# One relation of SBUF places, modulo 256 bytes, for the K steps of a float32 transformer layer

## The chip, the cores and the metric

The kernel runs on one core of one Trainium2 chip. The metric is the device time of one execution in microseconds: the median of three executions is 1042.79 us (1042.51 to 1045.53). TensorE (PE) multiplies, ScalarE (ACT) and VectorE (DVE) prepare operands, GpSimd (POOL) helps with elementwise work, SyncE (SP) issues most transfers. SBUF is the on-chip memory that the engines read, 128 partitions wide; a "place" in this document is the byte at which an operand starts within its partition.

## The reference, cut to what matters

One decoder layer over 272 tokens (16 meta tokens ahead of 256), model width 2048, all in float32:

```
p = h @ w_in                       -> q heads | kv latent | indexer q, k, weights | pool channels
A = sparse attention (top-64 keys of a lightning indexer, T5 bias, shared latent KV)
B = multi-scale causal pooling of the pool channels, a linear map per group, a scale
h = LN(alpha*h + concat(A, B) @ w_o)
z = conv3(h @ w_up) + b;  f = (gelu(z_a) * z_g) @ w_down          (w_up: 2048 x 11264, w_down: 5632 x 2048)
h = LN(alpha*h + f);  the 256 real tokens are returned
```

## The kernel before, in words

**Products in two parts.** Float32 values are split into an upper part (rounded to float32r by ACT) and a lower part (the rest, by DVE), and a product is three TensorE products: upper weights by upper activations, lower weights by upper activations, upper weights by lower activations. `product` (L256 to L265) does this for one block of 128 output columns: 16 K steps of 128 rows each, and in each step three matmuls, L263 (`wh`, `ah`), L264 (`wl`, `ah`), L265 (`wh`, `al`). A matmul holds a 128x128 weight block in the array (the trace shows its load as LDWEIGHTS on PEld, just before the matmul) and streams 256 to 272 activation columns past it. While one matmul streams, the block of the next one is loaded; so PE reads two places of SBUF at once: the activations of this matmul and the weights of the next.

**The stream of weights.** All weights come as tiles of 128 x 2048 floats in one fixed order, the list `stream`: items 0 to 7 are the indexer's queries, 8 and 9 the latent maps, 10 to 17 the query heads, 18 to 25 the pool channels, 26 to 41 the output projection, and from 42 on the plan of `ffn_plan`: 88 "up" items (one per block of 128 columns of `w_up`) with "down" items (`w_down`) between them. `fetch` (L162) brings an item by one DMA on SP into a `wraw` tile and splits it by two ACT (L158) and two DVE (L159) instructions into a `whl` tile. `wraw` and `whl` have three buffers each, so an item is fetched and split while PE uses those ahead of it. Down items go through `seven` (L849 on; matmuls L860 to L862), where activations are held in the array and 512 weight columns stream.

**Where operands lie.** A `whl` tile has 4352 floats, 17408 bytes, which is 68 x 256. The upper part starts at the first of `places(n)`, the lower at the second, both in floats from the tile's start; a step's block is 512 bytes behind the last, so it has the same place modulo 256. Activations of a K step (`xp`: the input, `mixa` and `mixp`: the mixers' outputs, `hp`: the normalised rows) lie in the `ring` pool in slots of 576 floats, 2304 bytes, 9 x 256. In the built program both pools start at 96 modulo 256, so the relation of two operands modulo 256 follows from the offsets alone.

- `places(n)` (L99) gives item n the upper place 4*(n % 16) floats, which is 16 bytes further for each item, and the lower one 2048 + s floats behind it, where s goes through `SHIFTS` = 0, 12, 24, 36, 52 as n // 16 goes up. For an up item n is its number among the up items plus 72 (`order_of`, L136 to L139); other items take their number in the stream.
- `Parts` (L82) puts an activation tile's upper part at float 0 and its lower at 272 for the first eight K blocks of the order `K_UP`, and at 2 and 276 for the last eight (`ACTS`). `xp` tiles are plain (L286): upper at 0, lower 288 floats behind; indexer queries read them from token 16, query heads from token 14, pool channels from token 0, 6, 10 or 12.

The first 8 up items use other activations, `fold` tiles (L728, 2080 bytes each, so that each starts 32 bytes further modulo 256 than the one before it), because the layer norm is folded in later. The 80 others use `hp`, of which 16 x 80 = 1280 K steps follow.

As an example: up item 71 has n = 143, so its upper weights lie at 4*15 = 60 floats and its lower 2048 + 36 floats behind; up item 87 has n = 159, upper again at 60 floats, lower 2048 + 52 behind.

Of the kernel before, what the change touches and what calls it, by code (L numbers as in the profile page):

```python
# [12 lines left out]
F32R = mybir.dt.float32r  # L13
# [68 lines left out]
class Parts:  # L82


    def __init__(self, slot, k):
        flat = slot.rearrange("p a b -> p (a b)")
        (a, b) = ACTS[k in K_UP[8:]]
        self.parts = flat[:, a:a + NQ], flat[:, b:b + NQ]

# [4 lines left out]
WIDE = 288  # L94
ACTS = ((0, 272), (2, 276))
SHIFTS = (0, 12, 24, 36, 52)


def places(n):  # L99

    upper = 4 * (n % 16)
    return upper, upper + 2048 + SHIFTS[n // 16 % 5]

# [7 lines left out]
def tile_layer(ctx, tc, xt, w_first, w_proj, w_uk, w_uv, w_pool, w_o, w_up, w_down, cols, rows, rel_bias, onehot, out):  # L111
# [23 lines left out]
    plan = ffn_plan()  # L135
    kinds, order_of, n_up = {}, {}, 0  # L136
    for item in plan:
        if item[0] == "up":
            order_of[len(stream)] = n_up + 72  # L139
            n_up += 1  # L140
            stream.append(w_up[item[2] * FT + item[1]])
        elif item[0] == "down":
            n = PARTS[FAST]
            stream.append(w_down[sum(PARTS[:FAST]) + n // 2 + (item[2] - 1) // 2 * (n // 4) + item[3]])
        else:
            kinds[len(stream)] = item[0]
            stream.append(w_down[sum(PARTS[:item[1]]) + item[2] * (PARTS[item[1]] // 2) + item[3]])
# [42 lines left out]
    def emit(i):  # L190
# [14 lines left out]
        if i == spare:  # L205
            raw = wp.tile([P, 2048], F32, tag="wraw", name="wraw")
            hl = Split(sb.tile([P, 4160], F32R, tag="y", name="whl_y"), 0, 2056)
        else:
            raw, hl = weight_tiles((0, 2112) if i > spare else places(order_of.get(i, i)))
        ready[i] = hl  # L210
# [61 lines left out]
    for k0, k1 in [(k, k + 1) for k in range(9)] + [(9, 12), (12, 15), (15, 16)]:  # L272
# [10 lines left out]
        for k in range(k0, k1):  # L283
            xk, wk, a0 = raw[:, k % 3, :T], raw[:, k % 3, T:], k % 6 // 3 * 1024 + k % 3 * MF
            c = slice(a0, a0 + MF)
            a = ring.tile([P, 2, T], F32R, tag="act", name="xp", padded_shape=[P, 2, WIDE])  # L286
            nc.scalar.activation(a[:, 0, :], xk, AF.Copy)
            nc.scalar.activation(hl[:, 0, c], wk, AF.Copy)
            nc.vector.tensor_tensor(a[:, 1, :], xk, a[:, 0, :].bitcast(F32), op=ALU.subtract)
            nc.vector.tensor_tensor(hl[:, 1, c], wk, hl[:, 0, c].bitcast(F32), op=ALU.subtract)  # L290
            x_parts.append(a)
            first.append((hl, c.start))
# [302 lines left out]
    def values(h, pts, ptx):  # L595
# [4 lines left out]
        nc.tensor.matmul(ps[:, 2 + P:NQ], vs[2][:, hs], pts[:, 2 * P:], start=False, stop=True)  # L600
        a = Parts(ring.tile([P, 2, WIDE], F32R, tag="act", name="mixa"), h)
        nc.scalar.activation(a[:, 0, :NQ], ps[:, :NQ], AF.Copy)
# [35 lines left out]
    def pooled(g, df, hl):  # L638
        for j in range(2):
# [6 lines left out]
            m = 2 * g + j  # L646
            a = Parts(ring.tile([P, 2, WIDE], F32R, tag="act", name="mixp"), 8 + m)
            nc.scalar.activation(a[:, 0, :NQ], ps[:, :NQ], AF.Copy, scale=col(G_POOL, m))
# [125 lines left out]
    def normalise(m):  # L774
        yd = y[:, m, Q0:]
        nc.vector.tensor_tensor(yd, yd, rs, op=ALU.mult)
        nc.vector.tensor_tensor(yd, yd, m2, op=ALU.add)
        nc.scalar.activation(yd, yd, AF.Identity, bias=col(LN1, 2 * m + 1), scale=col(LN1, 2 * m))
        a = Parts(ring.tile([P, 2, WIDE], F32R, tag="act", name="hp"), m)
        nc.scalar.activation(a[:, 0, :NQ], yd, AF.Copy)  # L780
        nc.vector.tensor_tensor(a[:, 1, :NQ], yd, a[:, 0, :NQ].bitcast(F32), op=ALU.subtract)  # L781
        h_parts.append(a)
# [377 lines left out]
```

## Time and profile before

| | us |
|---|---|
| median of three executions | 1042.79 |
| the profiled execution | 1042.49 |
| its span, first to last instruction | 1040.7 |
| PE busy in the span | 1033.0 |
| DVE busy | 890.9 |
| ACT busy | 620.6 |

Durations of PE matmuls overlap in the trace (one starts about 0.12 us behind the last and is shown for 0.28 us), so what a matmul costs is read from the distance between starts: in a timeline the first column is the start, the second the duration, both in us. One K step is the distance from one L263 to the next. In a table of windows each row is one stretch of time: its length, then each engine's busy time and number of instructions, the granted TensorE clock, the DMA engines' share and the rate in GB/s. The clock is a share of full speed there; over the whole span its mean is 0.997.

### The profile page before, as it was taken

Reading aid. Unit: us, or ns where it says so; the run is one execution under the profiler, and the core shown is the slowest. Engines: PE = TensorE matmul, PEld = TensorE weight load, DVE = VectorE, ACT = ScalarE, POOL = GpSimd, SP = SyncE. Lnnn points to the kernel's source line nnn. Section 1 sums busy time; section 2 is a strip of 40 time slices with the busy share of each in tenths; the row PEclk is TensorE's granted clock in tenths of the full one; section 3 lists DMA queues with packets and bytes.
Section 4 is the critical chain, followed back from the end, with each engine's and each line's share of the span. In section 5 each row is a group of like instructions: output and inputs, shape, how many; then the busy total and the mean of one; then the engine's idle time right before and its main releaser. Section 6 shows DMA issues by size and latency. Waiting matters only on the chain.

```text
span 1040.7 us, 19199 instructions
## 1 busy us (share of the span) xinstructions
PE 1033.0 (99%) x7644; PEld 983.8 (95%) x7644; DVE 890.9 (86%) x1401; ACT 620.6 (60%) x1000; POOL 185.5 (18%) x245
## 2 busy tenths in 40 slices
PE   9999999999999999999999999999999999999997
PEld 8999999999999999999999999999999999999986
DVE  6879668758779998888989989989998999989876
ACT  7656456645439845565656556565556565566665
POOL 1200014125320021120121101211112111120031
PEclk9999999999999999999999999999999999999998
DMA  9755643454554578978887788887888779887765
GB/s 326 261 186 194 236 144 132 135 200 162 185 181 140 190 224 242 282 282 288 287 270 266 275 291 273 277 266 270 298 274 278 263 276 287 277 273 269 286 214 161
DMA packets 59754, 250.28 MB, mean 240 GB/s; under 512 B 21734, under 2 KB 22416, under 8 KB 32656
## 3 DMA queue, kind: packets, MB, share of 16 engines
q1 hardware_dynamic: 34592, 230.42, 61.5%
q0 software_dynamic: 7888, 16.14, 8.2%
q10 hardware_dynamic: 17184, 2.49, 1.4%
q8 instruction: 60, 0.98, 0.4%
q14 instruction: 30, 0.25, 0.1%
HBM read 232.50 MB, written 2.11 MB: 225 GB/s over the span
## 4 chain that ended last, share of the span: by engine, by line
PE 94%; issue 2%; DMA 1%; DVE 1%; POOL 1%; ACT 0%; SPq 0%; POOLq 0%; DVEq 0%; ACTq 0%
PE mm L263 24%; PE mm L265 24%; PE mm L264 24%; PE at L861 6%; PE at L860 6%; PE at L862 6%; PE mm L336 2%; DMA wraw<-in_w_down 1%; DVE whl L159 1%; POOL gb L979 0%; PE mm L564 0%; DMA wraw<-in_w_first 0%; PE at L599 0%; PE at L425 0%; PE at L426 0%
## 5 line engine op out<-in xcount | busy, mean ns | idle before, releaser
L159 DVE TENSOR_TENSOR whl<-wraw,whl 128x1024 fp32r<-128x1024 f32 (+1 forms) x416 | 486.4, 1204 | 40.5 <-ACT whl L158 39.5
L158 ACT ACTIVATE whl<-wraw 128x1024 fp32r<-128x1024 f32 (+1 forms) x416 | 402.6, 1014 | 102.1 <-DMA wraw<-in_w_up 21.9
L263 PE MATMUL mm<-hp,whl 128*128 128x258 f32 x1280 | 362.4, 283 | 0.0
L264 PE MATMUL mm<-hp,whl 128*128 128x258 f32 x1280 | 361.5, 282 | 0.0
L265 PE MATMUL mm<-hp,whl 128*128 128x258 f32 x1280 | 361.5, 282 | 0.0
L264 PEld LDWEIGHTS mm<-hp,whl 128*128 128x128 f32 x1280 | 242.6, 190 | 3.1
L263 PEld LDWEIGHTS mm<-hp,whl 128*128 128x128 f32 x1280 | 242.1, 189 | 3.1
L265 PEld LDWEIGHTS mm<-hp,whl 128*128 128x128 f32 x1280 | 242.1, 189 | 0.4 <-DVE hp L781 0.2
L263 PE MATMUL mm<-xp,whl 128*128 128x256 f32 (+5 forms) x384 | 111.7, 291 | 0.0
L265 PE MATMUL mm<-xp,whl 128*128 128x256 f32 (+5 forms) x384 | 108.6, 283 | 0.0
L264 PE MATMUL mm<-xp,whl 128*128 128x256 f32 (+5 forms) x384 | 108.4, 282 | 0.0
L795 ACT ACTIVATE z<-mm,cv 128x256 f32<-128x256 f32 x40 | 22.6, 565 | 99.6 <-PE mm L265 99.6
L832 POOL TENSOR_TENSOR forms<-za 128x128 f32<-128x128 f32 x20 | 21.2, 1061 | 311.0 <-DVE za L813 244.5
L263 PEld LDWEIGHTS mm<-xp,whl 128*128 128x128 f32 x384 | 72.3, 188 | 0.6
L264 PEld LDWEIGHTS mm<-xp,whl 128*128 128x128 f32 x384 | 72.4, 188 | 0.4
L265 PEld LDWEIGHTS mm<-xp,whl 128*128 128x128 f32 x384 | 72.2, 188 | 0.5 <-issue 0.5
L795 ACT ACTIVATE za<-mm,cv 128x256 f32<-128x256 f32 x40 | 22.6, 565 | 83.4 <-PE mm L265 75.1
L861 PE MATMUL at<-whl,gp 128*128 128x512 f32 x180 | 70.8, 394 | 0.0
L862 PE MATMUL at<-whl,gp 128*128 128x512 f32 x180 | 70.6, 393 | 0.0
L860 PE MATMUL at<-whl,gp 128*128 128x512 f32 x180 | 69.2, 394 | 0.0
L835 POOL TENSOR_TENSOR forms<-za 128x128 f32<-128x128 f32 x20 | 20.3, 1016 | 199.9 <-DVE za L813 199.9
L862 PEld LDWEIGHTS at<-whl,gp 128*128 128x128 f32 x180 | 33.8, 188 | 7.7
(349 smaller groups left out, 1885.9 us busy)
## 6 DMA issues: line engine op xcount, KB each, us to landing
wraw<-in_w_up SPq DMA_DIRECT2D x88, 1024.0 KB, 5.1
wraw<-in_w_down SPq DMA_DIRECT2D x80, 1024.0 KB, 6.7
wraw<-in_w_proj SPq DMA_DIRECT2D x24, 1024.0 KB, 5.2
wraw<-in_w_o SPq DMA_DIRECT2D x16, 1024.0 KB, 4.9
y<-v POOLq DMA_DIRECT2D x27, 256.0 KB, 8.0
y<-u POOLq DMA_DIRECT2D x18, 256.0 KB, 4.9
wraw<-in_w_first SPq DMA_DIRECT2D x8, 304.0 KB, 5.3
x<-in_xt SPq DMA_DIRECT2D x1, 2176.0 KB, 8.2
```

Of the source, the lines that this page charges most:

```text
L158: upper = nc.scalar.activation(hl[:, 0, c], raw[:, c], AF.Copy)
L159: lower = nc.vector.tensor_tensor(hl[:, 1, c], raw[:, c], hl[:, 0, c].bitcast(F32), op=ALU.subtract)
L263: nc.tensor.matmul(ps, wh, ah, start=n == 0, stop=False)
L264: nc.tensor.matmul(ps, wl, ah, start=False, stop=False)
L265: nc.tensor.matmul(ps, wh, al, start=False, stop=n == KT - 1)
L336: nc.tensor.matmul(ps[:m, :T], hl[:, t // 2, a0 + a:a0 + a + m], x_parts[k][:, t % 2, :], start=k == 0 and t == 0, stop=k == KT - 1 and t ...
L795: nc.scalar.activation(z, src[:, 2:NQ], AF.Identity, bias=col(C_B, j), scale=col(C_W, 3 * j + 2))
L832: nc.gpsimd.tensor_tensor(s[:, 0], a21, a22, op=ALU.add)
L835: nc.gpsimd.tensor_tensor(s[:, 3], a11, a21, op=ALU.subtract)
L860: nc.tensor.matmul(ps, a[:, 0, i], hl[:, 0, w], start=j == 0, stop=False)
L861: nc.tensor.matmul(ps, a[:, 0, i], hl[:, 1, w], start=False, stop=False)
L862: nc.tensor.matmul(ps, a[:, 1, i], hl[:, 0, w], start=False, stop=j == n - 1)
```

## The change

`places` gives three fixed upper places instead of a sweep: 10 floats for items 0 to 7, 8 floats for items 8 to 25, 60 floats for all others, up and down items alike. The lower part is 2084 floats (8336 bytes) behind the upper one everywhere. `Parts` takes its offset and width as arguments: `xp` tiles now start at float 0, `mixa`, `mixp` and `hp` at float 2, and the lower part is always 274 floats (1096 bytes) behind the upper. The number, order, engine and size of all instructions and transfers stay as they are, and so do the tiles.

```
-        (a, b) = ACTS[k in K_UP[8:]]
-        self.parts = flat[:, a:a + NQ], flat[:, b:b + NQ]
+        self.parts = [flat[:, a:a + width] for a in (first, first + 274)]
...
-ACTS = ((0, 272), (2, 276))
-SHIFTS = (0, 12, 24, 36, 52)
+SHIFT = 36
+LATE, EARLY, QUERY = 60, 8, 10
...
 def places(n):
-    upper = 4 * (n % 16)
-    return upper, upper + 2048 + SHIFTS[n // 16 % 5]
+    upper = QUERY if n < 8 else EARLY if n < 26 else LATE
+    return upper, upper + 2048 + SHIFT
...
-            raw, hl = weight_tiles((0, 2112) if i > spare else places(order_of.get(i, i)))
+            raw, hl = weight_tiles((0, 2112) if i > spare else places(i))
...
-            a = ring.tile([P, 2, T], F32R, tag="act", name="xp", padded_shape=[P, 2, WIDE])
+            a = Parts(ring.tile([P, 2, WIDE], F32R, tag="act", name="xp"), 0, T)
...
-        a = Parts(ring.tile([P, 2, WIDE], F32R, tag="act", name="mixa"), h)
+        a = Parts(ring.tile([P, 2, WIDE], F32R, tag="act", name="mixa"), 2, NQ)
...
-        a = Parts(ring.tile([P, 2, WIDE], F32R, tag="act", name="hp"), m)
+        a = Parts(ring.tile([P, 2, WIDE], F32R, tag="act", name="hp"), 2, NQ)
```

`mixp` is changed like `mixa`, and the bookkeeping of `order_of` and `n_up` goes.

More of the change, by code (lines that the diff above doesn't have):

```diff
@@ L82, with __init__ @@
 class Parts:
-    def __init__(self, slot, k):
+    def __init__(self, slot, first, width):
         flat = slot.rearrange("p a b -> p (a b)")
-        (a, b) = ACTS[k in K_UP[8:]]
-        self.parts = flat[:, a:a + NQ], flat[:, b:b + NQ]
+        self.parts = [flat[:, a:a + width] for a in (first, first + 274)]
     def __getitem__(self, key):
@@ L135, in tile_layer @@
     plan = ffn_plan()
-    kinds, order_of, n_up = {}, {}, 0
+    kinds = {}
     for item in plan:
         if item[0] == "up":
-            order_of[len(stream)] = n_up + 72
-            n_up += 1
             stream.append(w_up[item[2] * FT + item[1]])
@@ L646, in pooled @@
             m = 2 * g + j
-            a = Parts(ring.tile([P, 2, WIDE], F32R, tag="act", name="mixp"), 8 + m)
+            a = Parts(ring.tile([P, 2, WIDE], F32R, tag="act", name="mixp"), 2, NQ)
             nc.scalar.activation(a[:, 0, :NQ], ps[:, :NQ], AF.Copy, scale=col(G_POOL, m))
```

## The prediction

> **What bounds the kernel now.** I read the page first, its busy times and its chain of waits.
>
> ```profile
> span 1040.7 us, 19199 instructions
> ...
> PE 1033.0 (99%) x7644; PEld 983.8 (95%) x7644; DVE 890.9 (86%) x1401; ACT 620.6 (60%) x1000; POOL 185.5 (18%) x245
> ...
> PE 94%; issue 2%; DMA 1%; DVE 1%; POOL 1%; ACT 0%; SPq 0%; POOLq 0%; DVEq 0%; ACTq 0%
> PE mm L263 24%; PE mm L265 24%; PE mm L264 24%; PE at L861 6%; PE at L860 6%; PE at L862 6%; PE mm L336 2%; DMA wraw<-in_w_down 1%; DVE whl L159 1%; POOL gb L979 0%; PE mm L564 0%; DMA wraw<-in_w_first 0%; PE at L599 0%; PE at L425 0%; PE at L426 0%
> ```
>
> PE is the bound: 94% of the chain, 72% of it in the three matmuls of a K step. So the question is how fast these run one behind the other. Windows over stretches that hold little else say that: query heads, output projection, the first eight up items on `hp`.
>
> ```profile
> 92.00:138.10 46.10, 46.10 (x386) 45.96 (x385) 30.47 (x61) 18.97 (x26) 0.00 (x0) 1.00 0.51 182
> 220.32:301.40 81.08, 81.08 (x677) 81.03 (x676) 61.39 (x72) 39.53 (x59) 33.11 (x31) 1.00 0.52 181
> 349.32:395.50 46.18, 46.18 (x386) 46.00 (x385) 42.96 (x82) 27.93 (x47) 8.75 (x13) 1.00 0.69 208
> ```
>
> The counts take in matmuls that only reach into a window. The first and third hold 8 products, 384 matmuls: 46.10 / 128 K steps is 360.2 ns a step, 46.18 / 128 is 360.8. The second holds 14 products, 224 steps: 81.08 / 224 is 362. The clock is at 1.00 and the load of weights fills all but a little of the time, yet PE never idles: what can change is only the rate of the steps. I call the mean of a step before 360.5 ns.
>
> **The change, its main part.** In bytes and modulo 256, weights less activations, the change fixes the three pairs that PE reads at once. While L264 streams (upper activations), the upper weights for L265 load: 240 - 8 = 232 for `hp` and the mixers, 40 - 64 = 232 for indexer queries (token 16 is 64 bytes in), 32 - 56 = 232 for query heads. While L263 streams, the lower weights load: 232 + 8336 gives 120. While L265 streams (lower activations, 1096 = 72 further), the next upper weights load: 232 - 72 = 160. So the triple is 120, 232, 160 in all 8 + 8 + 16 + 80 products.
>
> The trace of before holds this very triple once: the second half of up item 71 (upper weights at float 60, lower 2084 behind it, activations at floats 2 and 276). Here are the starts of its first step, its third, its last, and of what follows it:
>
> ```profile
> 850.10 0.28 PE L263 MATMUL mm<-hp,whl 128*128 128x258 f32 x1
> ...
> 850.81 0.28 PE L263 MATMUL mm<-hp,whl 128*128 128x258 f32 x1
> ...
> 852.54 0.28 PE L263 MATMUL mm<-hp,whl 128*128 128x258 f32 x1
> ...
> 852.89 0.39 PE L860 MATMUL at<-whl,right 128*128 128x512 f32 x1
> ```
>
> Two steps take 0.71 us, 355 ns each; then six take 2.08 us, 346.7 ns each. The half that is nearest to it is the second half of up item 87, whose upper weights and activations lie the same, and whose lower weights lie 64 bytes further (triple 184, 232, 160):
>
> ```profile
> 981.23 0.28 PE L263 MATMUL mm<-hp,whl 128*128 128x258 f32 x1
> ...
> 981.95 0.28 PE L263 MATMUL mm<-hp,whl 128*128 128x258 f32 x1
> ...
> 984.11 0.39 PE L860 MATMUL at<-whl,right 128*128 128x512 f32 x1
> ```
>
> Its last six steps take 2.16 us, 360 ns each. So the fast pace is not that of the place 232 alone. Is it a property of the triple, or an accident of one half? The query heads say which, since their places before were constant over all 16 steps:
>
> ```profile
> 94.83 0.28 PE L263 MATMUL mm<-xp,whl 128*128 128x258 f32 x1
> ...
> 97.66 0.28 PE L263 MATMUL mm<-xp,whl 128*128 128x258 f32 x1
> ...
> 103.45 0.28 PE L263 MATMUL mm<-xp,whl 128*128 128x258 f32 x1
> ...
> 106.33 0.28 PE L263 MATMUL mm<-xp,whl 128*128 128x258 f32 x1
> ...
> 109.21 0.28 PE L263 MATMUL mm<-xp,whl 128*128 128x258 f32 x1
> ```
>
> The first of these two (item 10) runs its second half at 2.83 / 8 = 354 ns, the other (item 13) both of its halves at 2.88 / 8 = 360. The two halves of item 13 use ring slots of other places modulo 512 and agree, so 256 is enough of a period, and a pace once found is kept. I take the fast pace as the triple's own: two steps of 355 ns, then 346.7.
>
> - **Up items**, 80 products of 16 steps: after, 2 x 0.355 + 14 x 0.3467 = 5.56 us; before, 16 x 0.3605 = 5.77. 0.21 us each, **16.6 us** together.
> - **Output projection**, 16 products, the same triple and almost the same pace before: 16 x 0.21 = **3.3 us**.
> - **Query heads**, 8 products at 360.2 before: 8 x 0.20 = **1.6 us**.
> - **Indexer queries**, 8 products, the triple again but only 256 columns, which the trace does not show with it. Bounds from the nearest product, item 4 of the stream:
>
> ```profile
> 50.86 0.28 PE L263 MATMUL mm<-xp,whl 128*128 128x256 f32 x1
> ...
> 51.57 0.28 PE L263 MATMUL mm<-xp,whl 128*128 128x256 f32 x1
> 51.91 0.28 PE L263 MATMUL mm<-xp,whl 128*128 128x256 f32 x1
> ...
> 53.67 0.28 PE L263 MATMUL mm<-xp,whl 128*128 128x256 f32 x1
> ```
>
> Its eight steps take 351 ns each, single ones 340 (0.34 us). With 128 steps, between 351 to 340 (a gain of 1.4 us) and 351 to 360 (a loss of 1.2) I take a gain of 0.5, nearer to the fast end since the triple was fast at 258 columns.
>
> Sum: 16.6 + 3.3 + 1.6 + 0.5 = **22.0 us**.
>
> **The change, what else it moves.** *Down items* now stream weights from places 240 and 128 instead of many. Their activations stay spread over many places. Two of their steps, a fast one and a slow one:
>
> ```profile
> 705.92 0.40 PE L860 MATMUL at<-whl,right 128*128 128x512 f32 x1
> ...
> 706.63 0.40 PE L860 MATMUL at<-whl,right 128*128 128x512 f32 x1
> ...
> 862.13 0.39 PE L860 MATMUL at<-whl,gp 128*128 128x512 f32 x1
> ...
> 862.81 0.39 PE L860 MATMUL at<-whl,gp 128*128 128x512 f32 x1
> ```
>
> 0.71 and 0.68 us. If all 252 steps went from the middle to one end, that is 252 x 0.015 = 3.8 us either way; since the activations keep their spread I take 0 and keep 1 us each way. The 8 folded up items (moving relation) and the 8 pool products (four relations, mostly other widths) have 256 steps; by 6 ns either way (360 against the 354 of item 10) 1.5 us, taken as 0.
>
> *Splitting.* ACT and DVE write `whl` at other places. The whole of them, and the split of item 71, which wrote just the new places:
>
> ```profile
> L158 ACT ACTIVATE whl<-wraw x416: 609/1049/1086, 20.6 to 1009.1; 128x1024 fp32r<-128x1024 f32 x127, 128x512 fp32r<-128x512 f32 x12
> ...
> L159 DVE TENSOR_TENSOR whl<-wraw,whl x416: 677/1219/1668, 21.7 to 1011.4; 128x1024 fp32r<-128x1024 f32 x127, 128x512 fp32r<-128x512 f32 x12
> ...
> 840.60 2.01 ACT L158 ACTIVATE whl<-wraw 128x1024 fp32r<-128x1024 f32 x2 [0.92 <-DMA wraw<-in_w_up]
> ...
> 841.69 2.63 DVE L159 TENSOR_TENSOR whl<-wraw,whl 128x1024 fp32r<-128x1024 f32 x2
> ```
>
> ACT takes 2.01 us for the pair, twice its median (least, median, most ns) less their overlap; DVE takes 2.63 against 2.44 for two medians. At worst each of the 168 up and down items costs DVE 0.2 us more, 34 us in all, which lies beside PE; I take 0 and keep it for the cover.
>
> *Cover.* A faster PE asks for weights sooner. One of the DVE splits with least time to spare ends 1.2 us ahead of its use:
>
> ```profile
> 859.92 2.35 DVE L159 TENSOR_TENSOR whl<-wraw,whl 128x1024 fp32r<-128x1024 f32 x2
> ...
> 863.50 0.28 PE L263 MATMUL mm<-hp,whl 128*128 128x258 f32 x1
> ...
> 0.00:23.00 23.00, 21.16 (x157) 19.78 (x158) 14.77 (x36) 16.02 (x36) 3.35 (x15) 1.00 0.93 344
> ...
> 400.00:700.00 300.00, 300.00 (x2134) 282.73 (x2134) 273.06 (x374) 176.88 (x248) 51.22 (x60) 1.00 0.83 276
> ```
>
> It waits for PE's own progress, and one up item of 0.21 us lies between: 1.0 us stays. DVE is busy 273 of 300 us, 91%; the feed-forward stage shrinks by 16.6 of 635 us, which makes 93.5% (some 98% with the 34 us on top). DMA goes from 276 to some 284 GB/s, and the first window shows 344. Both fit, DVE narrowly in the worst case. Were the cover gone, PE would go at DVE's pace, and the gain of the stage, 16.6 us, is the most that this could take.
>
> The sum against the profiled execution: 1042.5 - 22.0 = **1020.5 us**; the median of the runs, 1042.8, is 0.3 above it, which I leave aside.
>
> **A rule against it.** The Trainium skill, page "TensorE: Matmul & The Clock Gate", section "Step-by-step: what each phase is for", says that PE has two independent read ports and that loading the next weights takes nothing from the running matmul's reads. By that no place could matter and the sum would be 0; this is the second rival. The rows of item 71 against item 87 disagree with it by 13 ns a step.
>
> **Rivals.**
>
> 1. *A middle pace.* The one half was led in by its own first half, and coming from down items or from other columns, products settle at 354 (as item 10 did) or only some reach 346.7. For it: the single sample; against it: halves of constant places kept one pace. 1536 steps by 6.5 ns are 10 us: **1032.5**.
> 2. *Nothing.* Places do not set the pace; the half was the fastest of 160 by chance, and paces stay spread around 360. For it: selection of the best of many; against it: six equal steps in a row, and the two halves of item 13. **1042.5**.
> 3. *A slow pace, on the other side.* Each triple has several steady paces, and where a product enters decides. One entry now holds for all products, so a bad one is taken by all 1536 steps. The trace has such a pace, the first half of up item 11:
>
> ```profile
> 367.54 0.28 PE L263 MATMUL mm<-hp,whl 128*128 128x258 f32 x1
> ...
> 369.74 0.28 PE L263 MATMUL mm<-hp,whl 128*128 128x258 f32 x1
> ```
>
> 2.20 / 6 = 366.7 ns: 1536 x 6.2 = 9.5 us more, **1052**. It decides once more steps lie over 360.5 than under it. Against it: this triple shows 346.7 alone.
>
> **How the numbers follow.** Forecast 0.62, middle pace 0.19, nothing 0.11, slow pace 0.08. The forecast's own bounds: without settling steps 1536 x 8 ns x 2/16 = 1.5 us more gain, indexer queries 0.9, down items 1, folded and pool 1.5: 1016 if all fall well, and 1026 if all fall badly. To hold 8 in 10 the range must take in the middle pace: 1016 to 1034. Of this kernel a measurement can tell 0.3%, 3 us. Faster by more than that are forecast and middle pace, 0.81; within it is "nothing", 0.11; slower is the slow pace, 0.08.
>
> **What would show it.** Right: in a timeline of up items after, nearly all L263 stand 0.347 apart from the third step on, in both halves; a window of eight products on `hp` takes 44.5 us instead of 46.18; the window of query heads takes 44.5 instead of 46.10; PE stays over 98% busy, and no wait of PE for DVE or DMA appears. Middle: steps of 0.353. Wrong: steps that stay mixed around 0.360, or a pace over it; or PE idle ahead of up items with DVE's L159 as releaser, which would mean that the cover was too thin.

## The result and the profile after

The changed kernel takes 1036.09 us, median of four executions (1035.23 to 1038.21). Its ratio to the kernel before is 0.9938, 95% interval 0.9924 to 0.9953. So it is faster by 6.7 us between the medians, clear of the noise, where 22 were forecast, and it lies outside the range. The profiled execution is the longest of the four, 1038.21 us; sums over its trace are made against the 1042.49 us of the profiled execution before.

From the page after, the span, the busy times, and the chain of waits by engine and by line:

```profile
span 1036.4 us, 19199 instructions
...
PE 1027.3 (99%) x7644; PEld 978.3 (94%) x7644; DVE 890.3 (86%) x1401; ACT 621.5 (60%) x1000; POOL 188.4 (18%) x245
...
PE 94%; DMA 2%; issue 2%; POOL 1%; ACT 1%; DVE 0%; SPq 0%; POOLq 0%; ACTq 0%
PE mm L260 24%; PE mm L261 24%; PE mm L262 23%; PE at L858 6%; PE at L857 6%; PE at L859 6%; PE mm L333 2%; DMA wraw<-in_w_down 1%; DMA wraw<-in_w_first 0%; POOL gb L976 0%; PE mm L561 0%; PE at L596 0%; PE at L423 0%; PE at L422 0%; ACT whl L155 0%
```

Lines are 3 lower than before: the matmuls of a K step are L260 to L262, those of down items L857 to L859. The bound is the same. PE is 99% busy and 94% of the chain, and waits for DVE round to 0% of it. PE's busy time fell by 5.7 us, with the same 7644 matmuls.

The windows that the prediction read, at the places where these stages lie now (length, busy time and count of PE, PEld, DVE, ACT, POOL, clock, DMA share, GB/s):

```profile
93.30:139.50 46.20, 46.20 (x385) 46.03 (x384) 30.56 (x61) 19.06 (x26) 0.00 (x0) 1.00 0.51 181
222.00:303.20 81.20, 81.20 (x677) 81.14 (x676) 61.41 (x72) 39.50 (x59) 33.11 (x31) 1.00 0.53 181
351.30:397.40 46.10, 46.10 (x386) 46.10 (x385) 43.10 (x81) 27.84 (x47) 8.75 (x13) 1.00 0.69 207
```

Eight query heads still take 46.2 us, the output blocks 81.2, the first eight up items on `hp` 46.1: 360 ns a step, as before, where 44.5 us was forecast for the first and the last. Nothing was won here. Behind the first down items it looks different. From the timeline of PE, two up items that follow each other, with only a down item between; the first column is the start:

```profile
454.75 0.39 PE L859 MATMUL at<-whl,gp 128*128 128x512 f32 x1
454.98 0.28 PE L260 MATMUL mm<-hp,whl 128*128 128x258 f32 x1
...
455.68 0.28 PE L260 MATMUL mm<-hp,whl 128*128 128x258 f32 x1
...
460.19 0.28 PE L260 MATMUL mm<-hp,whl 128*128 128x258 f32 x1
...
460.54 0.39 PE L857 MATMUL at<-whl,right 128*128 128x512 f32 x1
...
462.62 0.28 PE L260 MATMUL mm<-hp,whl 128*128 128x258 f32 x1
...
463.34 0.28 PE L260 MATMUL mm<-hp,whl 128*128 128x258 f32 x1
...
468.02 0.28 PE L260 MATMUL mm<-hp,whl 128*128 128x258 f32 x1
...
468.38 0.40 PE L857 MATMUL at<-whl,gp 128*128 128x512 f32 x1
```

The first does just what was forecast: two steps of 350 ns, then 13 steps in 460.19 - 455.68 = 4.51 us, 347 each, and 5.56 us for the product. The second has the same triple of places, 120, 232, 160, the same instructions and the same clock, and takes 463.34 - 462.62 = 0.72 us for two steps, 360 each, and 4.68 us for the next 13, 360 again: 5.76 us for the product. Of the 80 up items on `hp` **32 go at 347 ns a step and 48 at 360**. Which one it is shows within the first four steps and then holds to the product's end.

| mean ns of one K step | before | after | steps |
|---|---|---|---|
| up items on `hp` | 360.4 | 355.5 | 1276 |
| output projection | 360.8 | 360.9 | 254 |
| query heads | 359.4 | 360.0 | 127 |
| indexer queries | 353.8 | 359.0 | 124 |
| pool channels | 373.4 | 376.4 | 112 |
| folded up items | 360.1 | 361.6 | 127 |
| down items | 694.8 | 694.5 | 335 |

(Steps whose three matmuls all stand in a row in the trace, without those of over 450 ns; means from distances of starts, which the trace holds to the nanosecond, while the views round to 10.) The up items gain 1276 x 4.9 ns = 6.3 us. The indexer queries give back 0.7, pool channels 0.3, folded items 0.2, query heads 0.1, and the first matmul of the stream starts 0.7 us later, at 23.8 us instead of 23.1. That leaves 4.3 us, which is the difference of the profiled executions.

### The profile page after: what moved, and what is told of

It reads as the page before. It is cut to its first block, busy times and chain, and to the rows that moved or that the text cites. A ratio compares the mean times of both kernels' runs of the same rounds, so it can differ in the third digit from the quotient of the medians.

```text
span 1036.4 us, 19199 instructions
## 1 busy us (share of the span) xinstructions
PE 1027.3 (99%) x7644; PEld 978.3 (94%) x7644; DVE 890.3 (86%) x1401; ACT 621.5 (60%) x1000; POOL 188.4 (18%) x245
## 4 chain that ended last, share of the span: by engine, by line
PE 94%; DMA 2%; issue 2%; POOL 1%; ACT 1%; DVE 0%; SPq 0%; POOLq 0%; ACTq 0%
PE mm L260 24%; PE mm L261 24%; PE mm L262 23%; PE at L858 6%; PE at L857 6%; PE at L859 6%; PE mm L333 2%; DMA wraw<-in_w_down 1%; DMA wraw<-in_w_first 0%; POOL gb L976 0%; PE mm L561 0%; PE at L596 0%; PE at L423 0%; PE at L422 0%; ACT whl L155 0%
## 5 line engine op out<-in xcount | busy, mean ns | idle before, releaser
L260 PE MATMUL mm<-hp,whl 128*128 128x258 f32 x1280 | 360.8, 282 | 0.0
L261 PE MATMUL mm<-hp,whl 128*128 128x258 f32 x1280 | 360.1, 281 | 0.0
L262 PE MATMUL mm<-hp,whl 128*128 128x258 f32 x1280 | 359.3, 281 | 0.0
L261 PEld LDWEIGHTS mm<-hp,whl 128*128 128x128 f32 x1280 | 243.2, 190 | 3.1
L260 PEld LDWEIGHTS mm<-hp,whl 128*128 128x128 f32 x1280 | 241.0, 188 | 3.2
L262 PEld LDWEIGHTS mm<-hp,whl 128*128 128x128 f32 x1280 | 241.5, 189 | 0.2
L260 PE MATMUL mm<-xp,whl 128*128 128x256 f32 (+5 forms) x384 | 112.3, 292 | 0.0
L261 PE MATMUL mm<-xp,whl 128*128 128x256 f32 (+5 forms) x384 | 109.0, 284 | 0.0
L262 PE MATMUL mm<-xp,whl 128*128 128x256 f32 (+5 forms) x384 | 108.9, 284 | 0.0
L829 POOL TENSOR_TENSOR forms<-za 128x128 f32<-128x128 f32 x20 | 21.8, 1092 | 302.4 <-DVE za L810 235.9
L261 PEld LDWEIGHTS mm<-xp,whl 128*128 128x128 f32 x384 | 73.0, 190 | 0.4
L260 PEld LDWEIGHTS mm<-xp,whl 128*128 128x128 f32 x384 | 72.3, 188 | 0.6
L262 PEld LDWEIGHTS mm<-xp,whl 128*128 128x128 f32 x384 | 72.3, 188 | 0.5 <-issue 0.5
L859 PE MATMUL at<-whl,gp 128*128 128x512 f32 x180 | 70.6, 393 | 0.0
L857 PE MATMUL at<-whl,gp 128*128 128x512 f32 x180 | 69.1, 394 | 0.0
L832 POOL TENSOR_TENSOR forms<-za 128x128 f32<-128x128 f32 x20 | 23.2, 1159 | 199.8 <-DVE za L810 186.3
L859 PEld LDWEIGHTS at<-whl,gp 128*128 128x128 f32 x180 | 33.9, 188 | 7.7
```

What stands on the lines that cost most here:

```text
L260: nc.tensor.matmul(ps, wh, ah, start=n == 0, stop=False)
L261: nc.tensor.matmul(ps, wl, ah, start=False, stop=False)
L262: nc.tensor.matmul(ps, wh, al, start=False, stop=n == KT - 1)
L829: nc.gpsimd.tensor_tensor(s[:, 0], a21, a22, op=ALU.add)
L832: nc.gpsimd.tensor_tensor(s[:, 3], a11, a21, op=ALU.subtract)
L857: nc.tensor.matmul(ps, a[:, 0, i], hl[:, 0, w], start=j == 0, stop=False)
```

## Experiments

The theory after this first look: a triple of places has **several steady paces**; which one a product takes is settled by how it is entered (what PE read just before, and how it was timed), and it is kept while the same triple goes on, into the next product too. The rival: the pace is the triple's own, and the 48 slow items are slow because of something that goes on beside them (DMA, DVE's writes, the buffer in use).

What went before the up items gave the first hint. 71 of the 80 are preceded by a matmul of a down item; in all but one of these its held activations lie in one of 16 slots (`gp`) of 2080 bytes, 32 bytes further modulo 256 from slot to slot. In the built program's addresses, with the slot's start modulo 256: slot at 192, 11 of 11 up items fast; at 128, 8 of 8 slow; the others mixed. The three `whl` buffers made no clear difference.

**One slot place for the down items' activations.** Slots of 2304 bytes instead of 2080, so that all 16 start alike: at 192 (first run, the "pinned slots" or "pinned version" from here on) or 128 (second). The `fold` tiles and the rows of the last norm share these slots and move with them. For the room, a `whl` tile goes from 4352 to 4224 floats, 66 x 256 bytes.

```
+GP = 56                                   # second run: 40
-    wp.tile([P, 4352], F32R, tag="whl", ...)
+    wp.tile([P, 4224], F32R, tag="whl", ...)
+    def gp_tile(name):
+        flat = fp.tile([P, 576], F32R, name=name, tag="gp", bufs=16)
+        return flat[:, GP:GP + 2 * NE].rearrange("p (a b) -> p a b", b=NE)
-            a = fp.tile([P, 2, NE], F32R, name="gp", tag="gp", bufs=16)
+            a = gp_tile("gp")
```

> The changed kernel, but all sixteen activation buffers of the down items get slots of a multiple of 256 bytes, so that what PE holds in the last step ahead of an up item always lies at 192 and 208 modulo 256 (whl tiles shrink by 512 unused bytes to make room; the folded items' activations lie there too). In the changed kernel all 11 up items that followed such a slot ran at 347 ns a step. Theory A (the triple has two steady paces, 347 and 360 ns, and the phase at the entry decides, which the last down step sets): at least 64 of the 71 up items behind a down item run at 347; against 32 that is some 34 items by 0.2 us, 7 us faster than the changed kernel, about 1029 us. Rival B (what runs beside, such as DMA, ACT and DVE, decides): about 32 fast items as now, 1036. Rival C (each entry is a draw by chance): about 32, 1036, and the fast ones others than before.

> As the run before, with the slots at 128 and 144 modulo 256. In the changed kernel all 8 up items that followed such a slot ran at 360 ns a step. Theory A (entry decides): at most 7 of the 71 up items behind a down item run at 347, and the gain over the kernel before is gone: about 1042 us. Rivals B (work beside) and C (chance): about 32 fast items, 1036.

At 192: 1026.14 us (1025.78 to 1028.96), ratio 0.9845 (0.9829 to 0.9862). At 128: 1036.53 us (1036.24 to 1040.18), ratio 0.9954 (0.9937 to 0.9971). In the first profile 69 of the 71 up items behind a down item are at 347; the nine ahead of the first down item stay at 360, and so do the output blocks and query heads. In the second, 22 of 80 are fast, where at most 7 were expected. One window over the middle of the feed-forward stage, 400 us, for the kernel before, the changed one, the slots at 192 and the slots at 128:

```profile
500.00:900.00 400.00, 400.00 (x2854) 377.54 (x2853) 367.16 (x507) 237.01 (x332) 65.31 (x78) 1.00 0.83 277
```

```profile
500.00:900.00 400.00, 400.00 (x2891) 377.29 (x2890) 371.84 (x513) 239.57 (x337) 66.78 (x80) 1.00 0.83 280
```

```profile
500.00:900.00 400.00, 400.00 (x2930) 377.32 (x2929) 376.37 (x520) 243.16 (x339) 66.60 (x80) 1.00 0.85 285
```

```profile
500.00:900.00 400.00, 400.00 (x2875) 377.26 (x2874) 368.91 (x510) 237.97 (x335) 65.41 (x79) 1.00 0.83 278
```

PE is busy for all of the 400 us in each, at the full clock; what differs is how many matmuls it gets through: 2854, 2891, 2930, 2875. DVE and DMA rise with PE (DVE to 376 of 400 us, DMA to 285 GB/s) and PE still waits for neither. The up items' own places are the same in the last three. So the entry decides, by 10 us between the two slot places, which are all that differs between these two programs. But the slot's place alone is not the rule: 21 of the 70 items behind a slot at 128 were fast. They are not scattered: from the 18th up item to the 76th it is the first and the third of every eight.

**The pinned slots without the change.** The same edit on the kernel before.

> The kernel before, with its spread of places, and only the activation slots of the down items pinned at 192 modulo 256 as in the first experiment. Theory A: the pinning alone gives nothing, since the entries differ in places anyway and almost no triple of before has a pace of 347: 1041 to 1044 us. Rival: the pinning itself speeds up the down items or the split, and the gain of the first experiment over the changed kernel, 10 us, is there as well: 1032.

1041.89 us (1041.25 to 1043.9), ratio 0.9996 (0.9987 to 1.0006). Pinning is worth nothing by itself; it selects among the paces that the places offer.

**The new places for the 80 up items alone.** On the kernel before:

```
-            ... else places(order_of.get(i, i)))
+            ... else (60, 2144) if order_of.get(i, 0) >= 80 else places(order_of.get(i, i)))
-        a = Parts(ring.tile(..., name="hp"), m)
+        a = Parts(ring.tile(..., name="hp"), None)      # always floats 2 and 276
```

> The kernel before, with the new places for the 80 up items on hp alone (weights at float 60, lower 2084 behind, hp at floats 2 and 276); query heads, indexer queries, output blocks and down items keep the places of before. Theory A: the whole gain of the change lies in the up items, at 347 behind some down items and at 360 behind others; since the down items' weights lie elsewhere the draw is another one, some 25 to 40 fast of 80: 1034 to 1038 us. Were part of the gain in the other stages, the time would lie nearer to 1042.

1034.36 us (1034.0 to 1035.59), ratio 0.9923 (0.9907 to 0.994); 45 of 80 at 347, 35 at 360. All of the gain is in the up items. Here the first up item goes at 360, its last step is stretched to 0.53 us, and the second to ninth are at 347; with the pinned slots the first item's last step is stretched to 0.52 us, and the next eight stay at 360. Between the profiled executions, 1034.0 and 1038.21 us, the 13 more fast up items make 2.6 us; the other 1.6 is what the new places elsewhere cost.

**Other triples.** Two runs put another single triple everywhere: parts 8192 bytes apart with the weights 248 past the activations (248, 248, 176), and parts 8400 bytes apart (184, 232, 160; this is the triple of item 87, at 360 in the trace of before).

```
-SHIFT = 36
-LATE, EARLY, QUERY = 60, 8, 10
+SHIFT = 0                                 # second run: SHIFT = 52, and 60, 8, 10 kept
+LATE, EARLY, QUERY = 0, 12, 14
```

> The changed kernel with another triple for all the same products: weights 248 past the activations, the weights' parts 8192 bytes apart, the activations' parts as they are (248, 248, 176). In the kernel before, the one half with this triple ran at 347 ns from its first step on. Theory A leaves two cases: this triple has 347 as its only steady pace (then all 112 products take it, some 1020 us), or it has two and the entries share them (1030 to 1040). Rivals B and C: as many fast items as now, about 1036.

> The changed kernel with the weights' parts 8400 bytes apart instead of 8336 and nothing else (triple 184, 232, 160). In the kernel before, the one half with it ran at 360. Theory A: the distance of the parts belongs to the triple, so this one has other steady paces: none at 347, the 80 up items near 360, 1041 to 1043 us. Rival (the entries alone matter, and any fixed triple does): 25 to 40 up items at 347, 1035 to 1038.

248, 248, 176: 1040.91 us over ten executions (1035.86 to 1043.15, in two groups, four at 1035.9 to 1036.5 and six at 1040 to 1043), ratio 0.9976 (0.9956 to 0.9995). Its profile, of an execution of the faster group, has up items at three paces: 37 at 347 (the nine ahead of the first down item among them), 2 at 353 and 41 at 367; 15 of 16 output blocks are at 347. Its eight query heads, with the same triple and the same 258 columns, do something else: steps of 352 and 362 ns in turn, all through. So the triple modulo 256 is not all that sets which paces there are. 184, 232, 160: one execution, 1035.09 us, 33 up items at 347, 47 at 360, 11 output blocks at 347. So 8336 bytes is not special; the triple that the prediction took as the slow contrast goes at 347 as often as the chosen one.

**Spread weights, or two places of activations.** Two runs undo half of the change each: weights swept through 80 places as before with the activations fixed (80 triples, one for each up item), and weights fixed with the activations of before (128, 240, 176 in the first eight steps, 120, 232, 160 in the last eight).

```
# first run                                # second run
-    upper = QUERY if n < 8 else ...       -        a = Parts(..., name="hp"), 2, NQ)
-    return upper, upper + 2048 + SHIFT    +        a = Parts(..., name="hp"), m)
+    upper = 4 * (n % 16)                  +ACTS = ((0, 272), (2, 276))
+    return upper, upper + 2048 + SHIFTS[n // 16 % 5]
```

> One part of the change alone: activations as changed (all hp, mixa and mixp at floats 2 and 276, xp at 0 and 274), weights at the spread places of before. So each of the 80 up items has one triple over all 16 steps, but 80 different ones; 10 of them have the upper weights 232 or 248 past the activations, as the triples had that showed 347 so far. Theory A1 (few triples have a pace of 347, and 232 and 248 with this distance of the activations' parts are among them): 2 to 8 of the 80 up items at 347, all of them among those ten; 1040 to 1043 us. Rival A2 (any triple that holds over a whole product has a pace of 347 as one of several, and the changes of the triple in mid-product kept PE from it): 25 to 40 up items at 347, spread over all places; 1034 to 1038 us.

> The other part alone: weights at the fixed places of the change, activations as before (floats 0 and 272 for the first eight K blocks, 2 and 276 for the last eight; xp with its parts 1152 bytes apart). So every product on hp has the triple 128, 240, 176 in its first half and 120, 232, 160 in its second, as up item 71 had it before. Theory A: the first halves run at the paces of their own triple (355 to 362), the second halves at 347 or 360 as the first half leaves them; if its pace is one and the same, all second halves fall alike: 80 x 8 x 13 ns = 8 us less, 1034, or nothing, 1042; with two paces between these. Rival A2 (a triple must hold over the whole product): hardly a half at 347, 1042.

Spread weights: 1041.07 us (1039.77 to 1043.51), ratio 0.9985 (0.9976 to 0.9995). Of 80 triples with one sample each, by the mean of steps 9 to 15, 54 go at about 360, 16 at about 353, 9 at 363 or more, and one at 347: it is the item with 120, 232, 160. The mean of all steps is 359.2 ns. Were a 347 as frequent in each of them as in the two single triples above, some 30 items would show it; so it is uncommon, but a sample of one per triple cannot tell which others have it: 184, 232, 160 shows 360 here, and had 33 fast items in the run above.

Two places of activations: 1038.53 us (1038.35 to 1041.07), ratio 0.9969 (0.9956 to 0.9982). 66 of 80 second halves are at 347, 14 at 360. From the timeline, one item of each kind; a K step starts with L264 in this kernel:

```profile
461.63 0.28 PE L264 MATMUL mm<-hp,whl 128*128 128x258 f32 x1
...
463.80 0.28 PE L264 MATMUL mm<-hp,whl 128*128 128x258 f32 x1
464.17 0.28 PE L264 MATMUL mm<-hp,whl 128*128 128x258 f32 x1
464.54 0.28 PE L264 MATMUL mm<-hp,whl 128*128 128x258 f32 x1
...
465.25 0.28 PE L264 MATMUL mm<-hp,whl 128*128 128x258 f32 x1
...
466.99 0.28 PE L264 MATMUL mm<-hp,whl 128*128 128x258 f32 x1
...
495.53 0.28 PE L264 MATMUL mm<-hp,whl 128*128 128x258 f32 x1
...
498.42 0.28 PE L264 MATMUL mm<-hp,whl 128*128 128x258 f32 x1
...
500.94 0.29 PE L264 MATMUL mm<-hp,whl 128*128 128x258 f32 x1
```

The upper item's first half runs into steps of 370 ns (463.80 to 464.17 to 464.54) and its second half then makes five steps in 1.74 us, 348 each. The lower item's first half takes 2.89 us for eight steps, 361 each, and its second half goes on with seven steps in 2.52 us, 360 each. Both halves' places are the same in both items. Item 71, the prediction's only sample, is the upper kind: the same two triples stand one after the other, its last two first-half steps take 358 and 367 ns, and then come 353, 354 and 346.

**An extra matmul at the entry.** A short matmul ahead of the first step of a product shifts the entry and nothing else; its output is overwritten by the step that follows. First with another width for each of eight query heads, 15 output blocks and eight up items:

```
+    def product(..., kick=0):
+            if kick and n == k0:
+                nc.tensor.matmul(ps[:, :kick], wh, act[k][:, 0, lo:lo + kick], start=True, stop=True)
-        product(ps[:, :NQ], hl, mix, 0, NQ, K_O, ...)
+        product(ps[:, :NQ], hl, mix, 0, NQ, K_O, ..., kick=16 * m)
```

> The changed kernel with one short extra matmul ahead of the first step of each query head, of each output block and of the first eight up items on hp; its result is overwritten, and its width goes through 16 to 240 (32 more each for the 8 query heads), 16 to 240 (16 more each, output blocks) and 24 to 248 (32 more each, up items). In the changed kernel all these products ran at 360 ns a step, each taking over the pace of the last. Theory A: some widths shift the phase so that the product goes to 347 and stays there, some leave it at 360; both paces are seen among these 31 products. Rival B (no fast pace in these stages because of what runs beside): all stay at 360. Each extra matmul costs 0.05 to 0.12 us, some 3 us in all.

One execution, 1039.17 us. All query heads stay at 360; output blocks with widths 32, 48, 80, 128 and 240 go at 347, the others at 360; so do up items with 56 and 152. Each costs 0.11 us, whatever its width (from its start to that of the second step 0.47 us, where a step alone takes 0.36), 3.4 us for all 31, more than the seven fast products gain. A disturbance of that size turns the pace of the 16 steps behind it, in some cases and not in others.

Then once per stage: 32 columns ahead of output block 2, 56 ahead of the second up item, none anywhere else.

> The changed kernel with two extra matmuls only, whose results are overwritten: one of 32 columns ahead of output block 2, and one of 56 columns ahead of the second up item on hp. Those widths led to 347 where every product had one. Theory A (a pace once taken is carried into the next product): output blocks 2 on and up items 9 to 16 on hp run at 347 with nothing further ahead of them, the blocks at least up to the next stall of PE (there is one ahead of block 5): 8 up items and 3 to 14 blocks by 0.2 us, 2 to 4 us in all. Rival (each product finds its own pace, and 360 is what these stages have): only the two products behind the extra matmuls are fast, 0.4 us.

One execution, 1033.04 us. All 14 output blocks from 2 on are at 347, through what stands ahead of block 5 as well, and so are the second to ninth up items. Starts of the first, second, third and ninth up item (K steps start with L262 here), with the extra matmul at L261:

```profile
348.39 0.28 PE L262 MATMUL mm<-hp,whl 128*128 128x258 f32 x1
...
354.14 0.19 PE L261 MATMUL mm<-hp,whl 128*128 128x56 f32 x1
354.17 0.36 PE L262 MATMUL mm<-hp,whl 128*128 128x258 f32 x1
...
359.84 0.28 PE L262 MATMUL mm<-hp,whl 128*128 128x258 f32 x1
...
393.12 0.28 PE L262 MATMUL mm<-hp,whl 128*128 128x258 f32 x1
```

The first takes 5.78 us, 360 ns a step and the extra matmul with it; from the third to the ninth it is 33.28 us for six products, 5.55 each, 347 a step. Nothing stands between the first item and the second but one matmul that costs 0.11 us, and in two executions of the changed kernel, which lacks it, all nine stay at 360: the pace is **carried from product to product**, since all have the same triple. What stands ahead of block 5 is no wait, as the expectation had it: PE computes a sum there, `ones` by `acc` (L743 in the changed kernel), without idling.

**Both together, four attempts.** The pinned slots with the triple 248, 248, 176 for the query heads, output blocks and first nine up items, because these had gone at 347 in its own run; then the pinned slots with the two extra matmuls and the old places for items 0 to 25:

> The pinned kernel (activation slots of the down items at 192 modulo 256), with the triple 248, 248, 176 for the query heads, the output blocks and the nine up items on hp ahead of the first down item, and 120, 232, 160 for all others. Theory A (the triple sets which steady paces there are, the entry picks one, and it is carried from product to product): output blocks and the nine up items at 347 instead of 360, query heads at 357, the 71 others at 347 as pinned. 15 x 16 + 9 x 16 = 384 steps by 13.3 ns are 5.1 us, query heads 0.4: 1026.1 - 5.5 = 1020.6 us. Rival B (work beside) or C (chance): no more fast products than the pinned kernel has, 1026.

> The pinned kernel (activation slots of the down items at 192 modulo 256, triple 120, 232, 160) with the two single extra matmuls (32 columns ahead of output block 2, 56 ahead of the second up item on hp), and with the places of before for the first 26 items and for xp, whose steps were some 5 ns shorter in the indexer queries and 3 ns in the pool channels. Theory A: 14 output blocks and 8 up items go from 360 to 347, 22 x 0.2 = 4.4 us; the first 26 items give 128 x 5 + 128 x 3 ns = 1.0 us: 1026.1 - 5.4 = 1020.7 us, if both entries fall as they did. If the entry into block 2 comes out at 360 as well, 1023.5; if neither takes, 1025. Rival (no carry): 1025.

1026.31 us (1025.29 to 1032.28), ratio 0.9854 (0.9824 to 0.9884); and 1026.76 us (1025.69 to 1027.78), ratio 0.985 (0.9837 to 0.9864). Neither comes to the 1020.6 or so expected. In the first, the profiled execution is the long one, and its starts tell why. The third and ninth up item where this triple stood everywhere, then the second and ninth in the combined kernel:

```profile
358.43 0.28 PE L260 MATMUL mm<-hp,whl 128*128 128x258 f32 x1
...
391.70 0.28 PE L260 MATMUL mm<-hp,whl 128*128 128x258 f32 x1
```

```profile
359.04 0.29 PE L265 MATMUL mm<-hp,whl 128*128 128x258 f32 x1
...
400.10 0.29 PE L265 MATMUL mm<-hp,whl 128*128 128x258 f32 x1
```

33.27 us for six products, 347 ns a step, against 41.06 us for seven, 367 a step: the same triple, entered differently. All 16 output blocks and these nine up items kept the slow pace there. In the second kernel, 14 output blocks go at 347; but the first up item had come in at 347 by itself, and the extra matmul, which was to bring the others there, turned them to 360.

Then, with all places as in the changed kernel, the pinned slots with both extra matmuls, and with the one ahead of the output blocks alone:

> The version with the pinned slots (1026.14 us, 69 of 80 up items on hp at 347 ns a step, output blocks all at 360), with the two extra matmuls of the run that turned output blocks 2 to 15 and up items 9 to 16 to 347, and with all places as in the changed kernel, so that the stream up to the first down item is that run's. If a pace is set at the entry and carried from product to product: output blocks 2 to 15 at 347 (14 x 16 x 13.3 ns = 3.0 us), the second to ninth up item too (8 x 0.2 = 1.6 us), the extra matmuls cost 0.2 us together: about 1021.8 us. If the entries before the first down item differ between executions: between 1021.8 and 1026, and the profile shows which products stayed at 360.

> The same with the extra matmul ahead of output block 2 alone. If the pace is carried: output blocks 2 to 15 at 347 and the nine up items ahead of the first down item at 360 as the first one was in both runs with places like these: 3.0 us less than the pinned version, about 1023.2 us. If the extra matmul ahead of the up items was not needed: 1021.4 us.

Both: 1028.68 us (1027.91 to 1029.17), ratio 0.9867 (0.9853 to 0.988). One: 1026.13 us (1025.11 to 1026.84), ratio 0.984 (0.9827 to 0.9853). The first lies above its expected range, 1021.8 to 1026; it has once more an up item that entered at 347 and was turned: second to ninth at 360. And its extra matmul ahead of output block 2 failed: blocks 2 to 4 stay at 360, and 347 begins at block 5. The second has 14 output blocks and 78 of 80 up items at 347, more than any profile up to then, and the time is still 3 us over the expected one. The expectation set off from the pinned version's median. Set off from its profiled execution, 1028.96 us, the account closes: output blocks 3.0 us and nine more up items 1.9 to the good, folded up items at 366.2 instead of 359.9 ns 0.8 to the bad, the query heads start 1.4 us later (94.2 against 92.8), which makes 2.7; it is 1028.96 - 1026.36 = 2.6.

**The same kernel a second time.** The pinned version and the changed kernel again, unchanged:

> The version with the pinned slots, unchanged, in a second profiled execution. The first took 1028.96 us, while its other runs took 1025.78 to 1026.20. If the entries ahead of the first down item (output blocks and the first nine up items) fall differently from execution to execution, this profile can come out near 1026 with some of these products at 347 ns a step, at 0.2 us each; behind down items the 69 fast up items should be the same ones, since the down items set the entry there. If the entries are the same in each execution: 1029 again, output blocks and first nine up items all at 360, and the other runs' 2.8 us lie elsewhere.

> The changed kernel, unchanged, in a second profiled execution. The first took 1038.21 us with 32 of 80 up items at 347, output blocks at 360; its other runs took 1035.23 to 1036.47. Entries that differ between executions: another number than 32, or output blocks at 347, and a time that follows it at 0.2 us a product. Entries that are the same each time: 32 again, the same ones, and 1038.

The changed kernel: 1038.1 us, and exactly the same 32 up items at 347. The pinned version: 1027.91 us, and this time output blocks from 5 on and all nine first up items came in at 347, with nobody's help. A window inside the output projection, of the first execution and of the second:

```profile
250.00:290.00 40.00, 40.00 (x336) 40.00 (x335) 33.75 (x39) 19.45 (x29) 19.65 (x17) 1.00 0.54 185
```

```profile
250.00:290.00 40.00, 40.00 (x349) 40.00 (x348) 35.17 (x39) 20.80 (x32) 21.02 (x18) 1.00 0.54 185
```

336 matmuls in 40 us, then 349, by one and the same program. Behind a down item the entry repeats: 69 of 69 items again. Ahead of the first down item it may differ from execution to execution. The place where the pace turns, the sum ahead of block 5 and the block's first matmul, looks the same in both, first and second execution:

```profile
238.89 0.60 PE L748 MATMUL at<-acc,ones 128*128 128x258 f32 x2
239.14 0.47 PE L261 MATMUL mm<-mixp,whl 128*128 128x258 f32 x1
```

```profile
240.15 0.60 PE L748 MATMUL at<-acc,ones 128*128 128x258 f32 x2
240.39 0.47 PE L261 MATMUL mm<-mixp,whl 128*128 128x258 f32 x1
```

What differs is the state before, and it hides **inside the 360 ns**, finer than the views show. From the first matmul of a step to the second, on to the third and to the next step, blocks 1 to 4 take 123, 119 and 118 ns in the first execution and 117, 124 and 119 in the second. With the triple 120, 232, 160, the same disturbance behind the same inner spacing ended alike each time that the traces hold it:

| disturbance | spacing before, ns | pace behind it | runs |
|---|---|---|---|
| sum ahead of block 5 | 123, 119, 118 | 360 | changed kernel twice, slots at 192 (first execution), slots at 128 |
| the same | 117, 124, 119 | 347 | slots at 192 (second execution) |
| the same | 119, 121, 120 | 347 | pinned, two extra matmuls |
| the same | 347 already | 347 | once per stage; pinned with old places for items 0 to 25; pinned, one extra matmul |
| 32 columns ahead of block 2 | 118, 124, 118 | 347 | once per stage; pinned with old places for items 0 to 25; pinned, one extra matmul |
| the same | 123, 119, 118 | 360 | pinned, two extra matmuls |
| 56 columns ahead of the second up item | 118, 124, 118 | 347 | once per stage; every product |
| the same | 347 already | 360 | pinned with old places; pinned, two extra matmuls |

(Spacings agree to 1 ns within a row.) This accounts for why the extra matmuls helped in one run and harmed in the next, and why an execution with fast output blocks can come without them. The fast products save 1.8 us in up items and 2.3 in output blocks, and yet the second execution is only 1.05 us shorter: folded up items again cost 0.8, the query heads start 1.3 us later (94.1), and the stretch from the last up item to the last matmul is 1.4 us longer (57.5 against 56.1), which would leave 0.6; the rest is not accounted for. In that last stretch are waits that the first did not have, one of them for a DVE split:

```profile
996.34 0.50 PE L1069 MATMUL mm<-whl,gp 128*128 128x512 f32 x1 [0.32 <-DVE whl L157]
```

The best of all is the pinned version, alone or with one extra matmul, 1026.1 us: 16.2 and 16.4 us below the kernel before in the same runs (1042.3 and 1042.5) and 10 below the changed one.

## Why the prediction was wrong

- **What bounds the kernel**: right. PE is 99% busy at the full clock, and only the pace of the K steps changed.
- **"I take the fast pace as the triple's own"**: this is the step that failed. The triple has a second pace, 360, and more products take that than 346.7: 48 of the 80 up items. The prediction had item 71 at 347 and no second sample of its triple; it concluded from the two equal halves of item 13 that a pace once found belongs to the places. What these halves show is that a pace is kept, from whatever entry (in the trace it is a pattern of 356, 367 and 357 ns that goes on). That the first half handed its pace to the second was the other reading, and the runs with one extra matmul and with two places of activations show that paces are handed on.
- **Item 87 as the contrast**: 184, 232, 160 at 360 against 120, 232, 160 at 347 was taken as proof that the triple sets the pace. It was one entry of each; 184, 232, 160 has both paces too.
- **Size of the fast product**: right, 5.56 us forecast and 5.56 measured, 0.2 us below a slow one. The term of 80 x 0.21 us was right in its size and wrong in its count: 32 products in the changed kernel. With 69 to 78 of them fast the stage from the first up item on `hp` to the last matmul goes from 686.7 us to 671.3 and 669.2, 15.4 and 17.5 less; 16.6 was forecast.
- **Output projection and query heads**, 3.3 and 1.6 us: nothing. All 16 and all 8 go at 360. The output blocks' 3.0 us could be had by an entry; the query heads went at 360 with eight different entries, and no run found a faster one that lasted with this triple.
- **Indexer queries**: a loss of 0.7 us instead of a gain of 0.5, inside the bounds given.
- **Down items, splits, cover**: held. Down steps changed by 0.3 ns in the mean, and PE did not come to wait for DVE in the stage, even when it went through 2930 matmuls in 400 us. Two side sums are off without consequence: with the 34 us on top DVE's share comes to 99%, not 98, and the slow bounds that are listed add up to 1024.7, not 1026.
- **The rivals**: the third had the mechanism, several steady paces and an entry that decides, at a chance of 0.08. It had the wrong consequence: the entry is not one for all products, since down items of 16 slots stand between them, and the other pace is 360, about what the mean was before, rather than 366.7. So the mixture gains. Within the first rival stood "only some reach 346.7", which is what happened, at fewer products than its 1032.5 us assumed. "This triple shows 346.7 alone" was an argument from one half of one item.

The Trainium skill, page "TensorE: Matmul & The Clock Gate", section "Step-by-step: what each phase is for", has loading the next weights take nothing from the running matmul's reads. What the prediction drew from it, that no place could matter, does not hold here: at a granted clock of 1.00 up items with the same instructions take 347 or 360 ns a step (367 with another triple), and the place of the preceding product's operand alone made 69 or 22 of 80 fast. Whether it is the loading that takes the time, no run here shows.

## What to carry to other kernels

One fast sample in a trace shows that a state can be reached, not that it belongs to the setting in which it was seen: look for what led it in, and count how many different entries the evidence covers before multiplying by the number of products. Equal neighbours are no second sample where a state is handed on. When PE is fully busy and matmuls of one shape still differ by a few per cent, compare distances of starts product by product; if they fall on a few values, look at what precedes each product, and make that preceding operand's place constant too. Equal lengths can still be different states: compare the distances inside a step before calling two products alike.

## What the runs showed of the hardware

- With one fixed triple, the steady K steps of up items and output blocks (three matmuls of 258 columns with a weight load each) fall on few lengths: 346.7, 353.3, 360.0 and 366.7 ns, 6.67 apart. Among the 80 triples of the spread weights there are also repeating patterns of two to five steps, with means in between, and the query heads with 248, 248, 176 alternate between 352 and 362.
- A triple of places modulo 256 of streamed and loaded operands offers up items some of these: 120, 232, 160 and 184, 232, 160 showed 347 and 360; 248, 248, 176 showed 347, 353 and 367.
- A product of a fixed triple mostly settles within two to four steps and keeps its pace through the products that follow; in three runs also through the sum ahead of output block 5 (14 blocks in a row).
- An extra 56-column matmul, which costs 0.11 us, moved the next 128 steps by 13 ns each. The place of an operand in the preceding product did the same for up items.
- Behind down items the outcome repeated exactly in a second execution (32 of 32, 69 of 69); ahead of the first down item it did so in the changed kernel and did not in the pinned version.
- Steps of 360 ns occur with several inner spacings of their three matmuls (118, 124, 118; 123, 119, 118; 119, 121, 120), and what a disturbance leads to differs with the spacing before it.
- Open: by what rule the entry decides, behind down items above all, and why the inner spacing of output blocks 1 to 4 differs between executions. The slot's place told part of it in the changed kernel (11 of 11 at 192, 8 of 8 at 128, the others mixed), but with all slots at 128, 21 of 70 came in fast. Whether 256 bytes is the true period was not tried.
